# A two-layer encoder trunk in split float32: column strips, float32 attention, a second DMA queue, more raw weight buffers, other groups

## The chip, the cores and the metric

One core of a Trainium2 chip runs the whole program. The metric is the device time of one execution in microseconds (us), lower is better. Engines: PE (TensorE), DVE (VectorE), ACT (ScalarE), POOL (GpSimd) and SP (SyncE, which here only issues DMAs). They run side by side and meet at semaphores.

## What is computed

Two layers of a hybrid encoder on one sequence of 1024 positions with 1024 channels, all float32, then a final RMSNorm. Cut to what matters:

```python
for layer in range(2):
    hn = rmsnorm(h, norm1_g[layer])
    u, q, k, v, gate_a, gate_b = split(hn @ w_in[layer])      # 512, 512, 128, 128, 1024, 1024 columns
    y_a = s5_branch(u, ...)        # bidirectional diagonal state space, 32 groups of 16 channels, then GLU
    y_b = windowed_gqa(q, k, v, sink, bias, mask)   # 8 heads of 64, 2 kv heads, window +-128, blocks of 128
    merged = sigmoid(gate_a) * (y_a @ w_branch_a) + sigmoid(gate_b) * (y_b @ w_branch_b)
    h = h + merged @ w_out[layer]
    hn2 = rmsnorm(h, norm2_g[layer])
    h = h + (silu(hn2 @ w_gate) * (hn2 @ w_up)) @ w_down      # 2816 hidden columns
return rmsnorm(h, final_g)
```

## The kernel before

**Tiling.** Activations lie with channels on the 128 partitions and the sequence in two halves of 512 columns (`HC`). A matrix product is a chain (`chain`, lines 167 to 176): for each 128x128 piece of the weights three matmuls of 512 columns, high weight by high activation (line 174), high by low (175), low by high (176). High and low are the float32r halves of a float32 number; ACT makes the high one by a copy, DVE the low one by a subtraction (`split`, lines 111 and 112; for weights `parts`, lines 162 and 163). A product of two plain float32 tiles is one instruction in the code and two records in the trace.

**Weights.** A granule is one weight tile of up to 128x1024. `fetch` (lines 120, 123) loads it into one of two `raw` buffers, `parts` or `quad_part` (lines 137 to 151) splits it into `whi` and `wlo`. `emit` walks the list of work items in the order of the code and brings the granules ahead of the items that use them; `ahead` fetches up to one granule beyond the one being split. A raw buffer is free again when DVE has made the low half.

**Stages of a layer.** Projections (`pj`), with the S5 tables prepared between them; attention in 16 units (kv head, block of 128 queries): scores (`s`, line 790), a fused add-and-maximum on DVE (793), exponentials on ACT (797), a scaling on DVE, transposes on PE (`pt`, 818), values (`pv`, 830); the S5 recurrence over 16 pairs of groups (`s5x`, 939, and `s5y`, 981 to 984); the GLU (`glu`), the branch products (`br`), `wo`, and the feed-forward part. This last runs in groups of hidden tiles (`GROUPS`): all gate and up products of a group, then 16 down chains (`dn`), which add to `h`. `h` lies in DRAM as `hs` between groups: each down chain loads its piece (line 1205), DVE adds (1210), and the sum is stored again (1212) except in the last group of the last layer, where the squares for the last norm are summed instead. From hidden tile 10 of the first layer and 2 of the second on, gate and up are multiplied as one 2x2 block product with seven instead of eight parts (`quad_items`: `qx`, `qy`, `qv`, `qw`).

**S5 tables.** For each of 2 x 16 pairs `s5_prep_pair` makes the matrices `WB` and `CA` on DVE and, on PE, four transposes (`pswb`, line 628) and 8 float32 matmuls into a 32-partition strip of one PSUM tile (`psE`, lines 642 and 644: four of 112 columns, four of 16). Tables, `u`, gates (`th`), and the S5 output (`s5g`, four DMAs for each pair of pairs, line 1009) go to DRAM and come back later.

**Order.** Every DMA is on SP's queue, loads and stores together, in one order; an issue that waits holds back those behind it. All other tiles are in one pool of 90 slots of 2 KB per partition (`N_SLOTS`), PSUM in 8 tiles of 512 columns. The first items of layer 0 keep the order of the code on PE, DVE and ACT; behind them a scheduler may move instructions within an engine, and it also chooses the slots.

In attention before, queries are held as two tiles for each pair of heads, `qe` and `qo`, with high and low halves of one head on the two halves of the partitions, and keys as `kh` and `kl`, each doubled over both halves, so that a head's scores are two float32r matmuls over 128 rows. The values tile has high and low columns next to each other (`vt`), so that two matmuls for each key block, with the high and low probabilities, give 128 output partitions whose halves ACT and DVE add (lines 832 and 842).

Of the kernel before, what the change touches and what calls it, by code (L numbers as in the profile page):

```python
# [8 lines left out]
F32 = mybir.dt.float32  # L9
# [17 lines left out]
          ((0, 2), (2, 3), (5, 3), (8, 3), (11, 3), (14, 3), (17, 3), (20, 2)))  # L27
# [14 lines left out]
N_SLOTS = 90  # L42
# [4 lines left out]
W_BUFS = 3  # L47
TB_EARLY = 4
# [46 lines left out]
class Trunk:  # L95
# [19 lines left out]
    def fetch(self, g):  # L115
        if isinstance(g, QuadPart):
            if g.kind in "ab":
                i = "ab".index(g.kind)
                r = g.quad.raw[i] = self.pw.tile([P, DM], F32, tag="raw", name="raw", bufs=2)
# [452 lines left out]
    def s5_table_early(self, l, q):  # L572
        self.nc.sync.dma_start(self.sp[l][q][2], self.s5_table(l, q))

    def s5_prep_pair(self, l, q):
# [43 lines left out]
        for g in range(2):  # L619
            dst = bass.AP(tensor=sp[1].tensor, offset=sp[1].offset + g * 256, ap=[[HC, 64], [64 * HC, 2], [1, 256]])  # L620
            nc.sync.dma_start(dst, CA[64 * g:64 * g + 64].rearrange("p (r c) -> p r c", r=2))
# [9 lines left out]
        nc.sync.dma_start(sp[0], WBT)  # L631

        i = q % 4
        if i == 0:
            self.psE = self.PS("psE")
        BD = BD.rearrange("p (q d r m) -> p q d r m", q=4, d=2, r=2)[:, i]
        ca = CA.rearrange("p (r d c) -> p d r c", d=2, r=2)
        E = self.psE[32 * i:32 * i + 32]
        cc = [t.rearrange("p (d q h) -> p d q h", d=2, q=NPAIR)[:, :, q] for t in (p["Cr"], p["Ci"])]
# [3 lines left out]
        for k, (d, r) in enumerate(((0, 0), (0, 1), (1, 0), (1, 1))):  # L643
            nc.tensor.matmul(E[:, 112:128], lhsT=BD[:, d, r], rhs=cc[r][:, d], start=k == 0, stop=k == 3)
        if i == 3:
# [4 lines left out]
            nc.sync.dma_start(self.ed[l][q // 4], es[:, 0:240])  # L650
# [51 lines left out]
    def key_tiles(self, kn, kv, T):  # L702

        nc = self.nc
        s = slice(64 * kv, 64 * kv + 64)
        hh, ll = self.A(f"kh{kv}{T}", F32R), self.A(f"kl{kv}{T}", F32R)
        for o in (slice(0, 64), slice(64, 128)):
            nc.scalar.copy(hh[o], kn[T][s])
        for o in (slice(0, 64), slice(64, 128)):
            nc.vector.tensor_tensor(ll[o], kn[T][s], hh[s].bitcast(F32), SUB)  # L710
        self.kt[kv, T] = (hh, ll)

    def value_tiles(self, vn):
        nc = self.nc
        for T in range(2):
# [3 lines left out]
            for b in range(2):  # L719
                vt = self.A("vt", F32R)  # L720
                o = vt.rearrange("p (k s d) -> p k s d", s=2, d=64)
                src = pt[:, b * 256:(b + 1) * 256].rearrange("p (k d) -> p k d", d=64)
                nc.scalar.copy(o[:, :, 0], src)
                nc.vector.tensor_tensor(o[:, :, 1], src, o[:, :, 0].bitcast(F32), SUB)
                self.vt.append(vt)

    def tile_q(self, l, i, xs=None):
        nc = self.nc
        st = {}

        def done(h, ps):
# [6 lines left out]
            lo, up = slice(0, 64), slice(64, 128)  # L738
            for T in range(2):
                e, o = self.A(f"qe{i}{T}", F32R), self.A(f"qo{i}{T}", F32R)  # L740
                nc.scalar.copy(e[lo], qn[T][lo])
                nc.vector.tensor_tensor(e[up], qn[T][lo], e[lo].bitcast(F32), SUB)
                nc.scalar.copy(o[up], qn[T][up])
                nc.vector.tensor_tensor(o[lo], qn[T][up], o[up].bitcast(F32), SUB)
# [879 lines left out]
```

## Time and profile before

| | us |
|---|---|
| median of 3 runs (2749.10 to 2753.00) | 2750.16 |
| the profiled execution, own time | 2751.03 |
| its span, first to last instruction | 2749.2 |
| PE busy / DVE busy / ACT busy / POOL busy | 2651.0 / 1880.3 / 972.1 / 0.2 |
| mean granted TensorE clock, as a share of 2.4 GHz | 0.983 |
| DMA: bytes moved, mean rate | 365 MB by SP's queue, 134 GB/s |

A PE record's duration is longer than its turn, because matmuls overlap in the array; what counts is the distance from one start to the next. A row's "<-" names what ended the idle time before it.

### The profile page before, as it was taken

Reading aid. Unit: us, or ns where it says so; the run is one execution under the profiler, and the core shown is the slowest. Engines: PE = TensorE matmul, PEld = TensorE weight load, DVE = VectorE, ACT = ScalarE, POOL = GpSimd, SP = SyncE. Lnnn points to the kernel's source line nnn. Section 1 sums busy time; section 2 is a strip of 40 time slices with the busy share of each in tenths; the row PEclk is TensorE's granted clock in tenths of the full one; section 3 lists DMA queues with packets and bytes.
Section 4 is the critical chain, followed back from the end, with each engine's and each line's share of the span. In section 5 each row is a group of like instructions: output and inputs, shape, how many; then the busy total and the mean of one; then the engine's idle time right before and its main releaser. Section 6 shows DMA issues by size and latency. Waiting matters only on the chain.

```text
span 2749.2 us, 35031 instructions
## 1 busy us (share of the span) xinstructions
PE 2651.0 (96%) x12738; PEld 2182.3 (79%) x12738; DVE 1880.3 (68%) x3881; ACT 972.1 (35%) x1829; POOL 0.2 (0%) x4
## 2 busy tenths in 40 slices
PE   8999997899999999999999999999999999999996
PEld 6788876688788888888878888888877888878775
DVE  8977988674965666656675877756377566656656
ACT  5325754432322222222345653343233223212222
POOL 0000000000000000000000000000000000000000
PEclk9999998999999999999999999999999999999998
DMA  3453235354245342553342135534415433543453
GB/s 118 133 164 112 95 113 172 120 202 139 84 125 187 105 147 73 176 169 106 123 167 75 56 108 177 177 122 154 134 65 176 162 103 131 180 161 94 138 173 132
DMA packets 205053, 367.47 MB, mean 134 GB/s; under 512 B 22304, under 2 KB 70688, under 8 KB 204880
## 3 DMA queue, kind: packets, MB, share of 16 engines
q1 hardware_dynamic: 204880, 365.23, 40.4%
q8 instruction: 100, 1.64, 0.2%
q14 instruction: 73, 0.60, 0.1%
HBM read 246.70 MB, written 118.44 MB: 133 GB/s over the span
## 4 chain that ended last, share of the span: by engine, by line
PE 80%; DVE 11%; DMA 5%; ACT 2%; issue 2%; SPq 1%; DVEq 0%; ACTq 0%
PE pj L174 6%; PE pj L175 6%; PE pj L176 6%; PE dn L174 4%; PE dn L175 4%; PE dn L176 4%; DMA raw<-in_w_up 2%; PE qy L187 2%; PE qy L185 2%; PE wo L175 2%; PE wo L174 2%; PE wo L176 2%; PE qy L186 2%; PE qv L187 2%; PE qv L186 2%; PE qv L185 2%
## 5 line engine op out<-in xcount | busy, mean ns | idle before, releaser
L162 ACT CAST whi<-raw 128x1024 fp32r<-128x1024 f32 (+3 forms) x208 | 169.5, 815 | 540.4 <-DMA raw<-in_w_down 130.8
L163 DVE TENSOR_TENSOR wlo<-raw,whi 128x1024 fp32r<-128x1024 f32 (+3 forms) x208 | 193.3, 930 | 196.7 <-ACT whi L162 188.2
L174 PE MATMUL pj<-rah,whi 128*128 128x512 f32 x768 | 308.6, 403 | 7.9 <-DVE sm L793 6.8
L175 PE MATMUL pj<-ral,whi 128*128 128x512 f32 x768 | 303.0, 395 | 3.5 <-DVE ral L112 3.5
L176 PE MATMUL pj<-rah,wlo 128*128 128x512 f32 x768 | 302.0, 394 | 0.0
L1210 DVE TENSOR_TENSOR h<-h,dn 128x512 f32<-128x512 f32 x224 | 151.0, 684 | 139.5 <-PE dn L176 98.3
L174 PEld LDWEIGHTS pj<-rah,whi 128*128 128x128 f32 x768 | 146.1, 190 | 43.3 <-DVE sm L793 8.3
L175 PEld LDWEIGHTS pj<-ral,whi 128*128 128x128 f32 x768 | 146.2, 190 | 35.0 <-DVE ral L112 6.7
L176 PEld LDWEIGHTS pj<-rah,wlo 128*128 128x128 f32 x768 | 145.8, 190 | 31.1
L185 PE MATMUL qx<-rfh,whi 128*128 128x512 f32 x256 | 100.2, 391 | 2.3 <-ACT whi L150 2.3
L187 PE MATMUL qx<-rfh,wlo 128*128 128x512 f32 x256 | 100.3, 392 | 1.0 <-DVE wlo L151 1.0
L186 PE MATMUL qx<-rfl,whi 128*128 128x512 f32 x256 | 100.1, 391 | 0.0
L174 PE MATMUL wo<-mgh,whi 128*128 128x512 f32 x256 | 100.0, 391 | 0.0
L175 PE MATMUL wo<-mgl,whi 128*128 128x512 f32 x256 | 99.7, 390 | 0.1
L176 PE MATMUL wo<-mgh,wlo 128*128 128x512 f32 x256 | 99.7, 389 | 0.0
L967 ACT COPY s5sg<-s5s 64x256 f32<-64x256 f32 x128 | 51.7, 404 | 135.1 <-DVE s5s L962 120.8
L174 PE MATMUL dn<-ffbh,whi 128*128 128x512 f32 x216 | 85.1, 394 | 0.0
L175 PE MATMUL dn<-ffbl,whi 128*128 128x512 f32 x216 | 84.2, 390 | 0.0
L175 PE MATMUL dn<-ffal,whi 128*128 128x512 f32 x216 | 84.2, 390 | 0.0
L797 ACT ACTIVATE x<-x,sm 128x384 f32<-128x384 f32 (+1 forms) x128 | 73.8, 578 | 29.3 <-DVE sm L793 29.3
L176 PE MATMUL dn<-ffah,wlo 128*128 128x512 f32 x216 | 84.1, 389 | 0.0
L174 PE MATMUL dn<-ffah,whi 128*128 128x512 f32 x216 | 84.1, 389 | 0.0
(440 smaller groups left out, 6726.3 us busy)
## 6 DMA issues: line engine op xcount, KB each, us to landing
hs<-h SPq DMA_DIRECT2D x240, 256.0 KB
h<-hs SPq DMA_DIRECT2D x240, 256.0 KB
raw<-in_w_in SPq DMA_DIRECT2D x52, 512.0 KB
raw<-in_w_gate SPq DMA_DIRECT2D x44, 512.0 KB
raw<-in_w_up SPq DMA_DIRECT2D x44, 512.0 KB
g<-th SPq DMA_DIRECT2D x64, 256.0 KB
thr<-g SPq DMA_DIRECT2D x64, 256.0 KB
raw<-in_w_down SPq DMA_DIRECT2D x80, 192.0 KB
```

The source lines that it names most:

```text
L162: nc.scalar.copy(g.hi[:, :n], g.raw[:, :n])
L163: nc.vector.tensor_tensor(g.lo[:, :n], g.raw[:, :n], g.hi[:, :n].bitcast(F32), SUB)
L174: mm(ps, lhsT=wh, rhs=xh, start=k == 0, stop=False)
L175: mm(ps, lhsT=wh, rhs=xl, start=False, stop=False)
L176: mm(ps, lhsT=wl, rhs=xh, start=False, stop=k == n - 1)
L185: mm(ps, lhsT=wh, rhs=xh, start=start and k == 0, stop=False)
L186: mm(ps, lhsT=wh, rhs=xl, start=False, stop=False)
L187: mm(ps, lhsT=wl, rhs=xh, start=False, stop=k == len(xs) - 1)
L797: nc.scalar.activation(ex[h][:, :n], ex[h][:, :n], AF.Exp, scale=-1.0, bias=nm[:, h:h + 1], accum_out=su[:, h:h + 1])
L967: nc.scalar.copy(SG[64 * r:64 * r + 64, g * 256:(g + 1) * 256].rearrange("p (d n) -> p d n", d=2), Sv[64 * g:64 * g + 64, :, r])
L1210: V.tensor_tensor(x, x, ps, ADD)
```

## The change

It has five parts.

- **psE over column strips.** The psE matmuls of a pair are kept back until four pairs are ready; then they are issued together, so that matmuls that follow each other write four different strips of 32 output partitions.
- **Float32 attention.** Queries, keys, values and probabilities stay plain float32, without high and low. Scores of two heads are issued in turn, one on partitions 0 to 63, one on 64 to 127, into two PSUM tiles; values of two heads in turn into output partitions 0 to 63 and 64 to 127. `att_values` ends in two copies of 128x128.
- **Stores through GpSimd.** All stores to DRAM but the bias row and the output go by `nc.gpsimd.dma_start`; loads stay with SP.
- **Four raw buffers.** `raw` has four buffers in place of two, and `ahead` fetches up to three granules beyond the one being split. They take 8 KB more per partition; `N_SLOTS` goes from 90 to 86, which is 8 KB.
- **Other groups in the second layer.** (2, 3, 3, 3, 3, 3, 3, 2) hidden tiles become (2, 2, 3, 3, 3, 3, 3, 3).

```diff
-          ((0, 2), (2, 3), (5, 3), (8, 3), (11, 3), (14, 3), (17, 3), (20, 2)))
+          ((0, 2), (2, 2), (4, 3), (7, 3), (10, 3), (13, 3), (16, 3), (19, 3)))
...
-N_SLOTS = 90
+N_SLOTS = 86
+R_BUFS = 4
...
-        g.raw = self.pw.tile([P, DM], F32, tag="raw", name="raw", bufs=2)
+        g.raw = self.pw.tile([P, DM], F32, tag="raw", name="raw", bufs=R_BUFS)
...
-            self.fetch_to(min(self.split_ + 2, len(self.order)))
+            self.fetch_to(min(self.split_ + R_BUFS, len(self.order)))
...
-        for d, dst, win in ((1, slice(0, 112), slice(16, 128)), (0, slice(128, 240), slice(0, 112))):
-            for r in range(2):
-                nc.tensor.matmul(E[:, dst], lhsT=BD[:, d, r], rhs=ca[:, d, r, win], start=r == 0, stop=r == 1)
+            for d, dst, win in ((1, slice(0, 112), slice(16, 128)), (0, slice(128, 240), slice(0, 112))):
+                for r in range(2):
+                    for k, (bd, ca, _) in enumerate(self.taps):
+                        nc.tensor.matmul(self.psE[32 * k:32 * k + 32, dst], lhsT=bd[:, d, r], rhs=ca[:, d, r, win],
+                                         start=r == 0, stop=r == 1)
...
-            for w in range(2):
-                for a, e in spans:
-                    kk = self.kt[kv, a // 4][w]
-                    nc.tensor.matmul(ps[:, (a - k0) * P:(e - k0) * P], lhsT=q, rhs=kk[:, (a % 4) * P:(a % 4 + e - a) * P],
-                                     start=w == 0 and a == k0, stop=w == 1 and e == k1)
+            for a, e in spans:
+                for j, ps in enumerate(pss):
+                    r = slice(64 * j, 64 * j + 64)
+                    nc.tensor.matmul(ps[:, (a - k0) * P:(e - k0) * P], lhsT=q[r, (3 - oq) * P:(4 - oq) * P],
+                                     rhs=self.kt[kv, a // 4][r, (a % 4) * P:(a % 4 + e - a) * P], start=a == k0, stop=e == k1)
...
-            out.append(self.split(ps, "p"))
+            out.append(self.A("p"))
+            nc.scalar.copy(out[k], ps)
...
-            for w in range(2):
-                nc.tensor.matmul(ps, lhsT=v, rhs=pt[k][w], start=k == 0 and w == 0, stop=k == n - 1 and w == 1)
-        t = self.A("pvl")
-        nc.scalar.copy(t[0:64], ps[64:128])
+            for j in range(2):
+
+                nc.tensor.matmul(ps[64 * j:64 * j + 64, 0:256].rearrange("p (i q) -> p i q", i=2), lhsT=v, rhs=p[:, j],
+                                 start=k == 0, stop=k == n - 1)
...
-            nc.vector.tensor_tensor(y[hp, w], ps[0:64, c], t[0:64, c], ADD)
+            nc.vector.tensor_copy(self.yb[2 * kv + i, T][:, (3 - o) * P:(4 - o) * P], ps[:, i * P:(i + 1) * P])
...
-                nc.sync.dma_start(dst, t[:, g * 256 + k * P:g * 256 + (k + 1) * P])
+                nc.gpsimd.dma_start(dst, t[:, g * 256 + k * P:g * 256 + (k + 1) * P])
...
-                nc.sync.dma_start(self.hs[m, h], x)
+                nc.gpsimd.dma_start(self.hs[m, h], x)
```

On PE, in the projections of layer 0, where the first S5 tables are made. Before, one pair's matmuls stand behind its transposes:

```order
L176 MATMUL pj_1424<-rah,wlo 128x512
L628 MATMUL pswb<-cst,WB 128x128 x4
L642 MATMUL psE<-CA,BD 32x112 x4
L644 MATMUL psE<-Cr,BD 32x16
L644 MATMUL psE<-Ci,BD 32x16
L644 MATMUL psE<-Cr,BD 32x16
L644 MATMUL psE<-Ci,BD 32x16
L174 MATMUL pj_1501<-rah,whi 128x512
```

Now, behind the transposes of the fourth pair:

```order
L177 MATMUL pj_1578<-rah,wlo 128x512
L629 MATMUL pswb<-cst,WB 128x128 x4
L645 MATMUL psE<-CA,BD 32x112 x16
L649 MATMUL psE<-Cr,BD 32x16 x4
L649 MATMUL psE<-Ci,BD 32x16 x4
L649 MATMUL psE<-Cr,BD 32x16 x4
L649 MATMUL psE<-Ci,BD 32x16 x4
L175 MATMUL pj_1669<-rah,whi 128x512
```

The 32 matmuls of four pairs stand in one row, 16 of 112 columns and 16 of 16, and neighbours write different strips.

On PE, in attention of layer 0, one unit's scores. Before (`kh`, `kl` keys, `qe`, `qo` queries of an even and an odd head):

```order
L790 MATMUL s<-kh_2202,qe_714 128x384
L790 MATMUL s<-kl_2203,qe_714 128x384
L790 MATMUL s<-kh_2202,qo_715 128x384
L790 MATMUL s<-kl_2203,qo_715 128x384
L790 MATMUL s<-kh_2202,qe_832 128x384
L790 MATMUL s<-kl_2203,qe_832 128x384
L790 MATMUL s<-kh_2202,qo_833 128x384
L790 MATMUL s<-kl_2203,qo_833 128x384
L818 MATMUL pt<-cst,x 128x128 x8
```

Now (`kk` keys, `qn` queries):

```order
L177 MATMUL pj_2536<-rah,wlo 128x512
L774 MATMUL s<-kk_2157,qn_651 128x384 x2
L774 MATMUL s<-kk_2157,qn_743 128x384 x2
L820 MATMUL pv<-p,vt 64x256 x4
L805 MATMUL pt<-cst,x 128x128 x12
```

Eight float32r matmuls became four float32 ones, in pairs over two halves of the rows.

On SP, in the S5 part of layer 0 (`zd` the stored S5 output, `s5wbt`, `s5ca`, `s5tb`, `s5uk` the loads for one pair). Before:

```order
L919 DMA s5uk<-ud_321 128x2x128
L924 DMA s5uk<-ed_1_183 128x1x128 x2
L1009 DMA zd_324<-s5g 8x16x128 x4
L123 DMA raw<-in_w_glu 128x1024
L914 DMA s5wbt<-sp_8_0_110 128x512
L914 DMA s5ca<-sp_8_1_111 128x512
L914 DMA s5tb<-sp_8_2_112 128x512
L919 DMA s5uk<-ud_322 128x2x128
```

Now:

```order
L904 DMA s5uk<-ud_325 128x2x128
L909 DMA s5uk<-ed_1_183 128x1x128 x2
L124 DMA raw<-in_w_br_a 128x1024
L899 DMA s5wbt<-sp_8_0_110 128x512
L899 DMA s5ca<-sp_8_1_111 128x512
L899 DMA s5tb<-sp_8_2_112 128x512
```

The four stores of `s5g` have left the row; they stand on POOL, where before there was no DMA.

## Rows read from the trace of the kernel before

**Rows 1.** The page, part 1: busy us, share of the span, instructions.
```profile
PE 2651.0 (96%) x12738; PEld 2182.3 (79%) x12738; DVE 1880.3 (68%) x3881; ACT 972.1 (35%) x1829; POOL 0.2 (0%) x4
```
**Rows 2.** Waits of PE, whole span: us in total, times, longest.
```profile
PE s5x L939 <- DMA s5uk<-ud: 15.4, 3, 6.4
PE psn L301 <- DVE sqc L292: 10.5, 3, 6.1
PE qy L185 <- ACT whi L150: 9.3, 9, 2.5
...
PE pj L174 <- DVE sm L793: 6.8, 5, 1.9
...
PE glu L174 <- ACT zp0h L111: 4.1, 1, 4.1
...
PE dn L174 <- ACT whi L162: 3.2, 1, 3.2
```
**Rows 3.** Timeline of PE, psE in layer 0: start, us, records.
```profile
128.34 0.95 PE L642 MATMUL psE<-CA,BD 128*32 128x112 f32 x8
129.13 0.21 PE L644 MATMUL psE<-Cr,BD 128*32 128x16 f32 x2
...
129.46 0.50 PE L174 MATMUL pj<-rah,whi 128*128 128x512 f32 x1
```
**Rows 4.** Timeline, S5 of layer 0: two strips in turn, then full width.
```profile
442.12 1.10 PE L939 MATMUL s5x<-s5uk,s5wbt 128*64 128x128 f32 x16
...
446.24 0.39 PE L983 MATMUL s5y<-s5sg,s5ca 128*128 128x127 f32 x2
...
446.46 0.39 PE L984 MATMUL s5y<-s5sg,s5ca 128*128 128x127 f32 x2
```
**Rows 5.** Timeline of PE, one attention unit of layer 0.
```profile
247.73 0.33 PE L790 MATMUL s<-kh,qe 128*128 128x384 f32 x1
...
249.14 0.39 PE L830 MATMUL pv<-ph,vt 128*128 128x512 f32 x1
...
250.08 1.47 PE L818 MATMUL pt<-cst,x 128*128 128x128 f32 x12
```
**Rows 6.** Timeline, S5 of layer 0: SP's queue and PE.
```profile
445.44 2.54 SPq L1009 DMA_DIRECT2D zd<-s5g  x4
...
450.00 0.38 SPq L919 DMA_DIRECT2D s5uk<-ud  x1
...
455.29 1.98 PE L939 MATMUL s5x<-s5uk,s5wbt 128*64 128x128 f32 x16 [6.43 <-DMA s5uk<-ud]
```
**Rows 7.** Stretches: us, busy PE, PEld, DVE, ACT, POOL, PEclk, DMA share, GB/s.
```profile
450.00:470.00 20.00, 11.13 (x85) 9.27 (x85) 18.19 (x41) 7.62 (x17) 0.00 (x0) 0.79 0.69 223
...
2080.00:2110.00 30.00, 23.41 (x86) 17.51 (x85) 22.75 (x36) 10.26 (x19) 0.00 (x0) 0.89 0.81 271
```
**Rows 8.** Timeline, end of a down stage of layer 1: SP, DVE, PE.
```profile
2649.45 0.46 SPq L120 DMA_DIRECT2D raw<-in_w_up  x1
...
2651.49 6.90 SPq L1212 DMA_DIRECT2D hs<-h  x3
...
2656.03 0.69 DVE L137 TENSOR_TENSOR sm<-raw 128x512 f32<-128x512 f32 x1 [2.83 <-DMA raw<-in_w_up]
...
2658.66 0.50 PE L185 MATMUL qy<-tt1h,whi 128*128 128x512 f32 x1 [2.51 <-ACT whi L150]
```
**Rows 9.** Timeline, the last down group and the last norm.
```profile
2712.74 1.05 PE L301 MATMUL psn<-ones,sqc 128*128 128x1 f32 x8 [2.84 <-DVE sqc L292]
...
2718.34 2.07 PE L324 MATMUL psn<-cst,rs 128*128 128x128 f32 x8 [2.51 <-DVE rs L87]
...
2733.78 1.84 PE L301 MATMUL psn<-ones,sqc 128*128 128x1 f32 x8 [6.06 <-DVE sqc L292]
```
**Rows 10.** Groups of DVE: line, shapes, count, busy us, mean ns, idle before.
```profile
L112 DVE TENSOR_TENSOR pl<-pt,ph 128x512 fp32r<-128x512 f32 x88 | 55.5, 683 | 1.1 <-ACT ph L111 0.4
L842 DVE TENSOR_TENSOR yb<-pv,pvl 64x128 f32<-64x128 f32 x128 | 36.0, 282 | 3.8 <-ACT pvl L832 1.7
```

More of the change, by code (lines that the diff above doesn't have):

```diff
@@ L118, in fetch @@
                 i = "ab".index(g.kind)
-                r = g.quad.raw[i] = self.pw.tile([P, DM], F32, tag="raw", name="raw", bufs=2)
+                r = g.quad.raw[i] = self.pw.tile([P, DM], F32, tag="raw", name="raw", bufs=R_BUFS)
                 self.nc.sync.dma_start(r, g.quad.src[i])
             return
-        g.raw = self.pw.tile([P, DM], F32, tag="raw", name="raw", bufs=2)
+        g.raw = self.pw.tile([P, DM], F32, tag="raw", name="raw", bufs=R_BUFS)
         self.nc.sync.dma_start(g.raw[:, :g.n], g.src)
@@ L630, in s5_prep_pair @@
         nc.scalar.copy(WBT, ps)
-        nc.sync.dma_start(sp[0], WBT)
+        nc.gpsimd.dma_start(sp[0], WBT)
         i = q % 4
         if i == 0:
-            self.psE = self.PS("psE")
[L636 to L639, printed above, removed]
-        for d, dst, win in ((1, slice(0, 112), slice(16, 128)), (0, slice(128, 240), slice(0, 112))):
-            for r in range(2):
-                nc.tensor.matmul(E[:, dst], lhsT=BD[:, d, r], rhs=ca[:, d, r, win], start=r == 0, stop=r == 1)
-        for k, (d, r) in enumerate(((0, 0), (0, 1), (1, 0), (1, 1))):
-            nc.tensor.matmul(E[:, 112:128], lhsT=BD[:, d, r], rhs=cc[r][:, d], start=k == 0, stop=k == 3)
+            self.taps = []
+        cc = [t.rearrange("p (d q h) -> p d q h", d=2, q=NPAIR)[:, :, q] for t in (p["Cr"], p["Ci"])]
+        self.taps.append((BD.rearrange("p (q d r m) -> p q d r m", q=4, d=2, r=2)[:, i],
+                          CA.rearrange("p (r d c) -> p d r c", d=2, r=2), cc))
+        if i == 3:
+            self.psE = self.PS("psE")
+            for d, dst, win in ((1, slice(0, 112), slice(16, 128)), (0, slice(128, 240), slice(0, 112))):
[3 more added lines that the diff above has]
+                                         start=r == 0, stop=r == 1)
+            for n, (d, r) in enumerate(((0, 0), (0, 1), (1, 0), (1, 1))):
+                for k, (bd, _, cc) in enumerate(self.taps):
+                    nc.tensor.matmul(self.psE[32 * k:32 * k + 32, 112:128], lhsT=bd[:, d, r], rhs=cc[r][:, d],
+                                     start=n == 0, stop=n == 3)
         if i == 3:
@@ L702, in key_tiles @@
     def key_tiles(self, kn, kv, T):
-        nc = self.nc
-        s = slice(64 * kv, 64 * kv + 64)
-        hh, ll = self.A(f"kh{kv}{T}", F32R), self.A(f"kl{kv}{T}", F32R)
+        kk = self.kt[kv, T] = self.A(f"kk{kv}{T}")
         for o in (slice(0, 64), slice(64, 128)):
[L708 to L711, printed above, removed]
+            self.nc.scalar.copy(kk[o], kn[T][64 * kv:64 * kv + 64])
     def value_tiles(self, vn):
@@ L718, in value_tiles @@
                 nc.tensor.transpose(pt[:, b * P:(b + 1) * P], vn[T][:, b * P:(b + 1) * P], self.ident)
[L719 to L725, printed above, removed]
+            self.vt.append(self.A("vt"))
+            nc.scalar.copy(self.vt[T], pt)
     def tile_q(self, l, i, xs=None):
-        nc = self.nc
         st = {}
@@ L763, in done @@
             store[i, h] = self.pd.tile([P, HC], F32, name=f"g{l}_{m0}_{i}_{h}")
-            nc.sync.dma_start(store[i, h], th)
+            nc.gpsimd.dma_start(store[i, h], th)
         return self.proj(l, m0 + i, done)
@@ L836, in att_values @@
                 self.yb[2 * kv + i, T] = self.A(f"yb{kv}{i}")
-        w = slice((3 - o) * P, (4 - o) * P)
-        for h in range(4):
-            y = self.yb[2 * kv + h // 2, T]
-            hp = slice(64 * (h % 2), 64 * (h % 2) + 64)
-            c = slice(h * P, (h + 1) * P)
-            nc.vector.tensor_tensor(y[hp, w], ps[0:64, c], t[0:64, c], ADD)
+        for i in range(2):
+            nc.vector.tensor_copy(self.yb[2 * kv + i, T][:, (3 - o) * P:(4 - o) * P], ps[:, i * P:(i + 1) * P])
     def att_pairs(self, kv):
```

48 lines of the change are left out of this document (20 added, 28 removed).

## The prediction

> **What bounds the kernel now.** I read the page first: PE is busy for 2651.0 us of a span of 2749.2, DVE for 1880.3, ACT for 972.1, POOL for nothing [rows 1]. So an edit pays where it shortens PE's own work or takes away one of the few waits of PE; work taken from DVE or ACT pays only where PE waits for it. The waits of PE come next [rows 2]. The reader is to see that they are short and scattered: 15.4 us for loads of the S5 part, 10.5 for the sums of squares in the norms, 9.3 and 3.2 for weights of the feed-forward part, 6.8 for DVE in attention, 4.1 for the first GLU product. Then I read the timeline at each place that the diff touches, to see what one instruction costs and which queue or engine stands behind each wait.
>
> **The change part by part.** *psE.* One pair takes from 128.34 to 129.46, 1.12 us: 0.79 for four float32 matmuls of 112 columns, 0.33 for four of 16 [rows 3]. The 32 pairs take 36 us, nearly all on PE's path. What strips give can be read from the S5 part [rows 4]. The full-width float32 matmuls start 0.22 us apart for 127 columns. The eight of s5x, with 128 columns in two strips of 64 by turns, are over in 1.10 us including the drain of the last record (about 0.28), so they start some 0.11 apart: two strips in turn halve the price. Each matmul is two records that go to the same strip one behind the other, so if records start in the order in which they are written, only neighbours overlap, and four strips give no more than a halving. I take half of the 112-column part, 32 x 0.39 = 12.6 us, and a quarter of the small ones, 2.6 us, since these may be held by a cost per instruction. That is -15. The bounds are 0 and, with four strips at once, three quarters of 36, -27.
>
> The Trainium skill ("TensorE: Matmul & The Clock Gate", Part 3) says that tiles of the array work at the same time, and gives 2.38 times for three column strips. By that the saving would be about -21, an estimate; [rows 4] show two strips only and can't decide between this and a halving.
>
> *Scores.* Eight float32r matmuls of 384 columns take from 247.73 to 249.14, 1.41 us [rows 5]. Now there are four float32 matmuls. By [rows 4] a float32 matmul costs 0.22 us for 127 columns, so 0.66 for 384; four one after the other take 2.66, and 1.33 if the two halves of the rows work at the same time. There are 32 units with 88 key blocks, 29 full units in all: +36 us at one end, -2.5 at the other. No row of this trace shows two row halves in turn. The nearest is two column strips with the same kind of matmul in the same alternation [rows 4], so I take the overlap, -3 with the units that were split over two key tiles, and keep +36 as a rival.
>
> *Values.* Four matmuls of 512 columns take from 249.14 to 250.08, 0.235 each, two for each key block: 0.47 [rows 5]. Two float32 ones of 256 columns are 0.44 each, in turn on two column strips of 64 as in [rows 4]: 0.44 for both. That is 88 x 0.03, -2.5 us; without overlap it would be +36, which rows 4 speak against.
>
> *DVE and ACT in attention.* DVE loses the low halves of the probabilities, 55.5 us, and the 128 additions, 36.0 us, for 64 copies of about 0.28 [rows 10], and some splits of queries and keys. This is hidden behind PE except where projections wait for the maximum, 6.8 us over both layers [rows 2]. I take -4 (0 to -8): the last unit, with little beside it, keeps its chain.
>
> *Stores out of SP's queue.* In the S5 part of layer 0 the four zd stores sit in front of the next loads; their issue alone takes 2.54 us, the u load goes out at 450.00, and PE stands still for 6.43 us until 455.29 [rows 6]. Three such waits make 15.4 us [rows 2], and after them PE runs at half clock for a while (PEclk 0.79 in this stretch [rows 7]). With the stores on POOL the loads are not held. But DVE is busy for 18.19 of 20 us there while PE does 11.13 [rows 7]: DVE is next late, and most of the wait can become a wait for it. I take -10 (0 to -25).
>
> *Four raw buffers.* At the end of a down stage the load of an up tile goes out at 2649.45 and SP is then held for 6.90 us by three hs stores; DVE waits for the tile until 2656.03 and PE for its high half until 2658.66 [rows 8]. With fetches two granules earlier and no stores before them, the 9.3 and 3.2 us [rows 2] should go, and a few us at half clock behind them. I take -15 (-6 to -20).
>
> *Groups.* In the last group two tiles make a chain of six matmuls, 1.4 us by [rows 5], while DVE has an addition and a sum of 0.69 each [rows 8] and a split of weights for it. So DVE falls behind, and PE waits 2.84, 2.51 and 6.06 us [rows 9]. With three tiles a chain is 2.1 us. The first wait goes; the second is the short chain of the norm and stays; the third shrinks by the five chains behind it, 5 x 0.7. That is -6 (0 to -9). The price is a second group of two tiles early in the layer. The first such group has PE busy for 23.41 of 30 us at a DMA share of 0.81 [rows 7], because 16 pieces of h are loaded and stored in little time. A second one may lose as much: I take +4 (0 to +10).
>
> *POOL as a queue.* POOL does nothing now [rows 1], so no row prices a store there. SP needs 2.54 us for four [rows 6]. Where a store is soon read back, as S5 output before the GLU (4.1 us [rows 2], in each layer its own hand-over), a later landing is paid in full. I take +3 (-2 to +8). The 4 slots fewer I cost at nothing: attention gives up more tiles than that; where slots are short elsewhere, that belongs to the third rival.
>
> The sum is -15 -3 -2.5 -4 -10 -15 -6 +4 +3 = -48.5 us. It is made against the profiled execution's 2751.0, which stands 0.9 above the median of the runs: 2702 us.
>
> **The rivals.** *Row halves don't overlap.* Scores cost +36 instead of -3: 2702 + 39 = 2741. For it: no row shows them. Against it: the strips of rows 4.
>
> *GpSimd's queue is the bound.* This one ends slower. In a down stage with three tiles PE gives a sum every 2.1 us, with two tiles every 1.4. Nine groups of three and two of two store 16 pieces each. If a store holds POOL for c us, the queue falls behind by 144 x (c - 2.1) + 32 x (c - 1.4); the pieces hold their slots, and the chains behind wait. It eats the 48.5 us at c = 2.25; at 2.5 it costs 93 and gives 2795. Against it: SP issues such stores in well under 1 us (a quarter of 2.54 [rows 6]); POOL would have to be four times as slow. The rule of the Trainium skill that speaks for it is in "SBUF — State Buffer" (SBUF: two separate sides): DMAs from GpSimd have their descriptors written by software, which is locked out while DVE runs a mode that uses two ports. No row here shows it.
>
> *The waits stay.* DVE takes the place of the loads in S5, the DMA rate that of the queue in the down stages (share 0.81 [rows 7]), and fewer slots give something back. Then there remain -15 -3 -2.5 -2 of PE's work and attention, and -1.5 of the groups: -24, 2727.
>
> *More strips, no DVE bound.* Four strips overlap (12 more) and the S5 waits go whole (8 more): 2682.
>
> **How the numbers follow.** The forecast has 50 of 100 (its own range 2685 to 2722), the waits that stay 20, the row halves 12, the better case 9, GpSimd's queue 9. The range from 2676 to 2744 takes in all but the last and the edges of two others. About 0.2%, 5.5 us, is what a measurement of this kernel can tell from no change. Of the row halves' case a third lies within or above that. So faster 0.86, same 0.04, slower 0.10.
>
> **What would show it.** psE: the 32 matmuls of four pairs in about 2.6 us instead of 4.5. Scores: four matmuls in 1.3 us, not 2.7; values 0.44 for a key block. S5: no wait of s5x for s5uk, in its place waits of s5y for DVE's states. Feed-forward: no qy or dn wait for whi. The end: a third psn wait near 2.5 us. POOL: a distance between hs stores set by DVE, not by POOL itself. The prediction is wrong if PE's records in scores start 0.32 us apart without pairs, if POOL's issues run back to back through the down stages, or if the S5 part of layer 0 is as long as before.

## Result and profile after

| | before | after |
|---|---|---|
| median, us | 2750.8 (4 runs, 2749.1 to 2753.0) | 2681.3 (4 runs, 2678.4 to 2683.7) |
| ratio, 95% interval | | 0.9746 [0.9729, 0.9763] |
| span of the profiled execution | 2749.2 | 2680.9 |

The change saves 69.5 us where 48.5 were forecast; the time lies inside the range (2676 to 2744) and near its lower end. The page of after, parts 1 and 5; [rows 1] has the first line of before:

```profile
PE 2607.8 (97%) x12914; PEld 2119.6 (79%) x12914; DVE 1765.1 (66%) x3673; ACT 929.9 (35%) x1761; POOL 295.0 (11%) x524
...
L1197 POOL DMA_DIRECT2D hs<-h x192 | 104.5, 544 | 875.8 <-DVE h L1195 849.2
```

PE lost 43 us of busy time and DVE 115. POOL holds 192 stores of `h` for 0.54 us each, and nearly all its idle time in front of them ends with DVE's addition: DVE sets their distance, not POOL. That rules out the rival of GpSimd's queue, which needed 2.25 us for a store.

Some of PE's longest waits in after (us in total, times, longest), to be held against [rows 2]:

```profile
PE s5x L924 <- DVE s5a L934: 10.6, 1, 10.6
...
PE s5x L924 <- DVE s5a L935: 5.5, 1, 5.5
PE psn L302 <- DVE sqc L293: 5.4, 2, 3.0
PE glu L175 <- ACT zp3h L112: 4.0, 1, 4.0
PE qy L186 <- ACT whi L151: 3.5, 1, 3.5
```

The waits of s5x have another name and the same size, 16.1 against 15.4 us. The waits for split weights (12.5 us) shrank to one of 3.5, and the squares wait twice instead of three times.

Where the time went, by stage. Every border is the first or last start of a tile's matmuls in PE's timeline (first and last score, first GLU product, last `wo`, last down product):

| stage, us | before | after | difference |
|---|---|---|---|
| start to first score, layer 0 (half of the S5 tables) | 233.6 | 216.8 | -16.8 |
| attention, layer 0 | 144.2 | 142.1 | -2.1 |
| S5, layer 0: last score to first GLU product | 150.1 | 141.2 | -8.9 |
| GLU, branches, `wo`, layer 0 | 157.9 | 161.6 | +3.7 |
| feed-forward, layer 0 (other half of the tables) | 728.4 | 714.3 | -14.1 |
| layer 1 up to its last `wo` | 606.6 | 597.0 | -9.6 |
| feed-forward, layer 1 | 706.6 | 688.9 | -17.7 |
| last down product to the end | 21.8 | 19.0 | -2.8 |

psE in after, PE's timeline (start, us, records), where [rows 3] had one pair at a time:

```profile
144.00 0.97 PE L645 MATMUL psE<-CA,BD 128*32 128x112 f32 x32
...
144.98 0.28 PE L649 MATMUL psE<-Ci,BD 128*32 128x16 f32 x8
145.19 0.50 PE L175 MATMUL pj<-rah,whi 128*128 128x512 f32 x1
```

Four pairs are over in 1.19 us, where one alone took 1.12. Over the 32 pairs, from start to start, psE fell from 36.0 to 9.9 us: the bound that the prediction gave as -27, not the halving that it took.

One attention unit in after, beside [rows 5]:

```profile
260.78 1.56 PE L774 MATMUL s<-kk,qn 64*128 64x384 f32 x8
262.27 1.52 PE L820 MATMUL pv<-p,vt 128*64 128x256 f32 x12
263.72 1.53 PE L805 MATMUL pt<-cst,x 128*128 128x128 f32 x12
```

The four scores take 1.49 us from their start to the next tile's (1.41 before), the values of three key blocks 1.45, 0.48 a block (0.47 before). So both kinds of halves do overlap; without that the scores alone would take 2.66, an estimate from the 0.66 us of one [rows 4]. But PE wins nothing by them.

The end, PE's timeline, beside [rows 9]:

```profile
2643.65 0.95 PE L302 MATMUL psn<-ones,sqc 128*128 128x1 f32 x8
2649.32 1.16 PE L325 MATMUL psn<-cst,rs 128*128 128x128 f32 x8 [2.51 <-DVE rs L88]
...
2665.33 1.02 PE L302 MATMUL psn<-ones,sqc 128*128 128x1 f32 x8 [3.02 <-DVE sqc L293]
2668.78 2.08 PE L325 MATMUL psn<-cst,rs 128*128 128x128 f32 x8 [2.43 <-DVE rs L88]
```

The first wait (2.84) is gone, the second stays at 2.51, the third fell from 6.06 to 3.02.

### The profile page after: what moved, and what is told of

Same layout as the page of the kernel before. It is cut to its first block, busy times and chain, and to the rows that moved or that the text cites. A ratio compares the mean times of both kernels' runs of the same rounds, so it can differ in the third digit from the quotient of the medians.

```text
span 2680.9 us, 35600 instructions
## 1 busy us (share of the span) xinstructions
PE 2607.8 (97%) x12914; PEld 2119.6 (79%) x12914; DVE 1765.1 (66%) x3673; ACT 929.9 (35%) x1761; POOL 295.0 (11%) x524
## 4 chain that ended last, share of the span: by engine, by line
PE 87%; DVE 7%; DMA 3%; ACT 1%; issue 1%; SPq 0%; POOL 0%; DVEq 0%; ACTq 0%
PE pj L175 6%; PE pj L176 6%; PE pj L177 6%; PE dn L175 6%; PE dn L176 5%; PE dn L177 5%; PE wo L175 2%; PE qy L186 2%; PE qy L188 2%; PE wo L176 2%; PE wo L177 2%; PE qy L187 2%; PE qv L186 2%; PE qv L187 2%; PE qv L188 2%; PE qx L187 2%
## 5 line engine op out<-in xcount | busy, mean ns | idle before, releaser
L1197 POOL DMA_DIRECT2D hs<-h x192 | 104.5, 544 | 875.8 <-DVE h L1195 849.2
L780 DVE CUSTOM_DVE_ANT_0 x<-s,bias,nsink 128x384 f32<-128x384 f32 (+1 forms) x128 | 67.7, 581 | 89.2 <-PE s L774 89.2
```

The costliest lines, as they stand in the source:

```text
L780: V.tensor_tensor_reduce(out=x[:, :n], in0=ps[:, :n], in1=self.bias[hd][:, bo:bo + n], op0=ADD, op1=ALU.min, scale=-1.0, scalar=self.nsink ...
L1197: nc.gpsimd.dma_start(self.hs[m, h], x)
```

## Experiments

Stages of the runs, us, from the profiled executions, borders as above (e1 varies its order from place to place, so its stages aren't listed):

| | before | after | e2 | e3 | e4 | e5 | e6 | e7 | e8 | e9 | e10 | e11 | e12 |
|---|---|---|---|---|---|---|---|---|---|---|---|---|---|
| to first score | 233.6 | 216.8 | 230.8 | 216.1 | 216.3 | 216.5 | 216.1 | 230.7 | 217.0 | 216.7 | 216.4 | 216.1 | 216.6 |
| attention 0 | 144.2 | 142.1 | 142.1 | 142.1 | 142.0 | 142.0 | 142.1 | 142.1 | 142.0 | 125.9 | 125.9 | 125.8 | 125.9 |
| S5 0 | 150.1 | 141.2 | 141.7 | 141.2 | 142.9 | 144.0 | 141.6 | 143.7 | 136.7 | 151.1 | 144.3 | 142.7 | 147.3 |
| GLU to `wo` 0 | 157.9 | 161.6 | 161.7 | 161.5 | 159.0 | 159.6 | 162.3 | 157.6 | 156.4 | 157.5 | 156.3 | 157.4 | 157.5 |
| feed-forward 0 | 728.4 | 714.3 | 727.9 | 717.7 | 712.6 | 717.9 | 714.5 | 734.7 | 712.7 | 712.7 | 712.4 | 713.8 | 711.7 |
| layer 1 to `wo` | 606.6 | 597.0 | 593.8 | 593.8 | 596.0 | 600.7 | 597.0 | 600.6 | 593.8 | 593.8 | 593.8 | 593.4 | 597.6 |
| feed-forward 1 | 706.6 | 688.9 | 689.1 | 696.3 | 689.7 | 707.5 | 685.8 | 707.3 | 690.8 | 692.1 | 688.0 | 682.4 | 683.0 |
| end | 21.8 | 19.0 | 19.8 | 19.0 | 18.0 | 18.1 | 22.4 | 21.2 | 19.0 | 19.7 | 19.2 | 18.7 | 18.1 |

Two rows show how far a stage moves with no edit in it. Layer 1 up to its `wo` takes 597.0 us in after and 593.8 in e2 and e9. The difference lies in its first projections, before the first score: 68.6 us at a mean granted clock of 0.95 in after, 65.4 at 1.00 in the two others. And the feed-forward part of layer 1, with the same code in after, e2, e8 and e9, takes 688.9 to 692.1. So 3 us in one stage of one pair of runs show nothing by themselves.

### e1: the order of the strips

In the scores `j` is the half of the rows, in the values the half of the output; `kv` is the kv head, `ks` the strips that are issued in turn.

```diff
+            sets = {1: ((0, 1), (2, 3)), 2: ((0,), (1,), (2,), (3,))}.get(q // 4, ((0, 1, 2, 3),))
+            for ks in sets:
...
-                    for k, (bd, ca, _) in enumerate(self.taps):
+                        for k in ks:
+                            bd, ca, _ = self.taps[k]
...
+        ops = [(i, a, e, j) for i in range(2) for a, e in spans for j in range(2)]
+        if kv:
+            ops.sort(key=lambda o: o[3])
...
+        ops = [(k, j) for k in range(n) for j in range(2)]
+        if kv:
+            ops.sort(key=lambda o: o[1])
```

> The changed kernel, with the issue order of the strips varied from place to place inside one program, so that one trace prices them. psE of layer 0 (four batches of four pairs, 32 matmuls each): batch 1 four strips in turn as in the changed kernel, batch 2 two strips in turn and then the other two, batch 3 strip by strip, batch 4 as batch 1. Scores and values of the first kv head in turn as in the changed kernel; of the second, the two heads on one half of the rows come first, then the two on the other half, and the values of one output half come for all key blocks before the other half. Theory, turns: neighbours in the queue that use different strips overlap, and a float32 matmul's two records do not stand in the way. Then batches 1 and 4 take 1.2 us, batch 2 about 2.3, batch 3 about 4.5 (4 x 1.12, as four pairs before); scores of a full unit 1.3 us for the first kv head and 2.0 for the second (three turns of 0.66 in place of two), values of three key blocks 1.3 and 2.2 (five turns of 0.44 in place of three). Rival, free overlap: the array takes whatever strip is free from further back, and batching alone is enough; then batches 2 and 3 take 1.2 to 1.5 too, and both kv heads cost the same. Second rival, the forecast's: only neighbouring records overlap; then four strips can't take less than 2.2, and batches 1 and 2 cost the same.

2695.9 us, a single run; what counts here is one trace's prices. PE's timeline of e1: the first psE row of batch 2 and the product that follows the batch, the same of batch 3, then one unit of the first and one of the second kv head:

```profile
174.34 0.96 PE L648 MATMUL psE<-CA,BD 128*32 128x112 f32 x16
...
176.40 0.50 PE L175 MATMUL pj<-rah,whi 128*128 128x512 f32 x1
...
200.31 0.95 PE L648 MATMUL psE<-CA,BD 128*32 128x112 f32 x8
...
204.19 0.50 PE L175 MATMUL pj<-rah,whi 128*128 128x512 f32 x1
...
273.95 1.56 PE L778 MATMUL s<-kk,qn 64*128 64x384 f32 x8
275.44 1.52 PE L826 MATMUL pv<-p,vt 128*64 128x256 f32 x12
...
342.99 1.57 PE L778 MATMUL s<-kk,qn 64*128 64x384 f32 x8
344.48 2.00 PE L826 MATMUL pv<-p,vt 128*64 128x256 f32 x12
```

The scores of a unit whose keys lie in two tiles, of the first kv head and of the second:

```profile
244.29 1.58 PE L778 MATMUL s<-kk,qn 64*128 64x256 f32 x16
...
331.87 2.34 PE L778 MATMUL s<-kk,qn 64*128 64x128 f32 x16
```

Four strips in turn take 1.19 us, two 2.06, strip by strip 3.88, each from the first start of the batch to the start of the next product. The price goes with the number of strips in turn, and the batching by itself brings little (4 x 1.12 = 4.48 against 3.88). That is the theory of turns, and the halving is out. But turns alone are not all: scores in the order half A, A, B, B cost the same as A, B, A, B (1.57 and 1.56 us), where three turns would have made 2.0, and the values by halves cost 2.00, less than the expected 2.2. A scheduler may move instructions here, but in the program of e1 PE's order in these units is that of the code. So a matmul on a free half of the array also starts ahead of one that waits in front of it, as far as one matmul back at least. It doesn't reach four back, since four on A and then four on B cost 2.34 us where in turn they cost 1.58, nor eight, or batch 3 would cost 1.2.

### e2: psE pair by pair

```diff
-                    for k, (bd, ca, _) in enumerate(self.taps):
-                        nc.tensor.matmul(self.psE[32 * k:32 * k + 32, dst], lhsT=bd[:, d, r], rhs=ca[:, d, r, win],
-                                         start=r == 0, stop=r == 1)
...
+        E = self.psE[32 * i:32 * i + 32]
...
+                nc.tensor.matmul(E[:, dst], lhsT=BD[:, d, r], rhs=ca[:, d, r, win], start=r == 0, stop=r == 1)
```

> The changed kernel with the psE matmuls issued pair by pair again, each pair in its own strip, as in the kernel before; all else as changed. Theory: the strips take psE from 36.0 to 9.9 us on PE and all of it lies on the path, so undoing it costs 26 us: 2681 + 26 = 2707, ratio to the kernel before 0.984. The forecast's step gave 15 (to 2696); and if PE would wait for something else in that time (tables that DVE is late with, or loads) less than 10 would come back, 2690.

2710.3 us, ratio to before 0.9848 [0.9828, 0.9867]. That is 28 us above after by the ratios, 26 by the spans. The stages show it where the tables are made, +14.0 up to the first score and +13.6 in layer 0's feed-forward part. All 26 us of psE lay on the path.

### e3, e4, e5: raw buffers and the stores' queue

e3 has the first of these edits, e4 the second (at every store), e5 both.

```diff
-R_BUFS = 4
+R_BUFS = 2
...
-                nc.gpsimd.dma_start(self.hs[m, h], x)
+                nc.sync.dma_start(self.hs[m, h], x)
```

> The changed kernel with two raw buffers in place of four and fetches one granule ahead; 86 slots as changed. Theory of the forecast: early fetches take away PE's waits for split weights in the feed-forward part (qy and dn for whi, 12.5 us in the kernel before) and some half clock behind them; undoing costs 15 us (6 to 20), 2681 + 15 = 2696, and qy and dn waits for whi come back. Rival: what held the loads was the stores in SP's queue ahead of them; with these on GpSimd two buffers are enough, and undoing costs 0 to 4 us, 2681 to 2685.

> The changed kernel with every store back in SP's queue; four raw buffers as changed. Theory of the forecast: the waits of s5x for loads in the S5 part of layer 0 come back (15 us in the kernel before) in place of its waits for DVE (16 us in the changed kernel), so the part gets only a little longer, and GpSimd's own price goes: net +7 us, 2688. Rival one: stores in SP's queue also hold the raw loads at the ends of the down stages, and four buffers don't cover it: +20, 2701, with qy or dn waits for whi. Rival two: stores on GpSimd bring nothing but a later hand-over of the S5 output to the GLU (waits for zp0h and zp3h, 5.9 us in the changed kernel): -5, 2676.

> The changed kernel with both queue parts undone: two raw buffers and every store in SP's queue; psE, attention, groups and 86 slots as changed. The S5 part of layer 0 (end of the last score to the first GLU product) took 150 us before, 141 in the changed kernel, 141 with two buffers alone undone and 143 with the stores alone undone. Theory, either is enough: the two parts cover for each other, so with both undone the part goes back to 150 us, s5x waits longer for its loads, and the total is 8 (raw buffers in the feed-forward part) + 9 above the changed kernel, 2698 to 2700. Rival: the 9 us come from the attention part (DVE and ACT with less behind them, more free slots) or from DVE being the bound in every case; then the part stays at 141 to 143 and the total is 2688 to 2691.

| | two raw buffers | four |
|---|---|---|
| stores on SP | e5: 2706.7, 0.9837 [0.9822, 0.9851] | e4: 2679.4, 0.9737 [0.9723, 0.9752] |
| stores on GpSimd | e3: 2689.8, 0.9774 [0.9759, 0.9789] | after: 2681.3, 0.9746 [0.9729, 0.9763] |

e3 lies between its theory (2696) and its rival (2681 to 2685), e4 between its theory (2688) and its second rival (2676). Both parts together are worth 25 us (0.0091 of 2751). Four buffers alone bring all of it (27); the stores alone bring 17; beside four buffers the stores bring nothing that these runs show. So they cover for each other, as e5's theory had it, but not in the S5 part, which it named: there the four kernels take 141.2 to 144.0 us, all below 150. Most of it, 18.6 us, lies in the feed-forward part of layer 1: 707.5 us with both undone, 696.3 and 689.7 with one, 688.9 with none. PE's waits of e5, then of e3:

```profile
PE s5x L924 <- DMA s5uk<-ud: 16.0, 4, 6.1
PE qx L186 <- ACT whi L151: 8.7, 2, 4.8
PE qy L186 <- ACT whi L151: 8.0, 8, 1.4
...
PE dn L175 <- ACT whi L163: 4.2, 3, 2.3
```

```profile
PE s5x L924 <- DMA s5uk<-ud: 16.8, 2, 10.6
...
PE qy L186 <- ACT whi L151: 5.6, 1, 5.6
```

The waits of qx, qy and dn for split weights are 20.9 us in e5. And s5x waits 16 to 17 us in all of them (in e4 13.0, and 4.4 for `zd`), under whatever name.

### e6: the old groups

```diff
-          ((0, 2), (2, 2), (4, 3), (7, 3), (10, 3), (13, 3), (16, 3), (19, 3)))
+          ((0, 2), (2, 3), (5, 3), (8, 3), (11, 3), (14, 3), (17, 3), (20, 2)))
```

> The changed kernel with the groups of the second layer as before, (2, 3, 3, 3, 3, 3, 3, 2). Forecast: the last group of three tiles saves 6 us at the end, the second group of two costs 4 early; undoing costs 2 us, 2683, with psn waits for the squares 3 and 6 us long again at the end. Rival: the second small group costs nothing, since with four raw buffers its loads are early; then undoing costs 6 to 9, 2687 to 2690. Other rival: the small group costs more than the end gives, and undoing is a gain, 2676 to 2680.

2681.4 us, ratio 0.9747 [0.9732, 0.9762]: no difference. Behind the last down product the old groups are 3.4 us slower (22.4 against 19.0), where PE waits longer for the squares again (5.4 us in after). Up to there they are 3.1 faster (685.8 against 688.9), which agrees with the forecast's early price but is no more than this part's spread:

```profile
PE psn L302 <- DVE sqc L293: 10.2, 3, 5.7
```

### e7: float32 attention alone

The kernel before with `key_tiles`, `value_tiles`, `tile_q`, `att_scores`, `att_transpose` and `att_values` of the changed kernel, and nothing else of it.

> The kernel before with the float32 attention alone (keys, values, queries, scores, probabilities, values; 90 slots, two raw buffers, stores in SP's queue, psE by pair, old groups). Forecast's steps: scores -3, values -2.5, less waiting for DVE -4, together -9.5: 2750 - 9.5 = 2741, and the S5 part of layer 0 as long as before (150 us from the last score to the first GLU product). Rival: the lighter attention also leaves DVE and ACT less behind when the S5 part begins, and the S5 part's 9 us come from here: 2732, S5 part 141 us. Rival, PE's work alone: only the matmuls get shorter, the waits stay: -5, 2745.

2738.7 us, ratio 0.9955 [0.9940, 0.9970], -12.4. In layer 0 attention itself gets 2.1 us shorter; 2.9 come before it, and 6.4 behind it, in the S5 part; layer 1 up to its `wo` gets 6.0 shorter. Two windows of 20 us around the last unit, before and e7 (length; busy PE, PEld, DVE, ACT, POOL; PEclk, DMA share, GB/s):

```profile
380.00:400.00 20.00, 17.10 (x77) 13.66 (x76) 13.29 (x37) 9.75 (x25) 0.00 (x0) 0.83 0.47 159
```

```profile
375.00:395.00 20.00, 19.49 (x123) 15.37 (x121) 14.25 (x39) 8.89 (x22) 0.00 (x0) 1.00 0.43 145
```

Before, PE stood for 2.9 us at the last unit's chain and then ran part of this stretch at the lower of its two clock levels, 1.2 GHz (mean 0.83); in e7 0.5 us of that wait is left and the clock stays at 1.00. Not explained: e7 gives 6 us back in layer 0's feed-forward part (734.7 against 728.4); PE's waits account for 3.0 of them.

### e8: the S5 part, and a releaser that misleads

In after the profile names DVE as what s5x waits for. SP's queue says otherwise. Timeline of after, SP and PE:

```profile
404.26 1.17 SPq L909 DMA_DIRECT2D s5uk<-ed  x2
421.55 0.34 SPq L124 DMA_DIRECT2D raw<-in_w_br_a  x1
...
423.41 0.38 SPq L904 DMA_DIRECT2D s5uk<-ud  x1
...
428.94 1.97 PE L924 MATMUL s5x<-s5uk,s5wbt 128*64 128x128 f32 x16 [5.51 <-DVE s5a L935]
```

From 405.4 to 421.55 SP issued nothing: a weight load stood at its head and waited for a raw buffer, and the loads of the next pair stood behind it. The u load went out at 423.41 and s5x started 5.5 us later; in before that took 5.3 [rows 6]. That DVE ends at that moment looks like a coincidence: in e3, where the S5 part takes the same time, the waits of s5x carry the load's name. SP's waits in this part, first of before (418 to 500 us), then of after (395 to 475 us):

```profile
SPq L1009 <- DVE s5g L1004: 25.1, 4, 15.2
SPq L123 <- DVE wlo L163: 4.0, 1, 4.0
```

```profile
SPq L124 <- DVE wlo L164: 34.7, 2, 18.6
```

Before, SP stood 25.1 us because the zd stores waited for DVE's result, not for the 2.54 us that their issue takes. In after a weight load that waits for DVE's split has taken their place. Both hang on DVE, which has a stall of its own. DVE's timeline of after:

```profile
432.23 0.68 DVE L981 SCALAR_TENSOR_TENSOR s5w<-s5g,s5y 128x512 f32<-128x512 f32 x1
434.39 0.69 DVE L989 SCALAR_TENSOR_TENSOR s5g<-s5g,s5y 128x512 f32<-128x512 f32 x1 [1.47 <-ACT s5g L982]
434.99 0.68 DVE L932 TENSOR_TENSOR s5a<-s5x,s5tb 128x512 f32<-128x512 f32 x1
```

DVE makes ACT's input and at once waits for ACT's tanh, with the next pair's states behind it. e8 puts them in between:

```diff
-            if end:
-                self.item(lambda i=i - 2: self.s5_store(i, st))
             if out:
                 self.item(lambda i=i - 1: self.s5_output(l, i, st))
             if on:
                 self.item(lambda q=2 * j: self.s5_states(l, q, st[q]))
+            if end:
+                self.item(lambda i=i - 2: self.s5_store(i, st))
...
+        if l == 0:
+            self.dve_order = range(first, len(self.seq))
```

In that range of items, layer 0's S5 part, DVE keeps the order of the code. The moved store and the kept order were not run apart.

> The changed kernel with another order on DVE in the S5 part of layer 0: the last multiplication of the S5 output (line 989) stands behind the states of the next pair and no longer directly behind the product that ACT's tanh waits for (line 981), and DVE keeps the order of the code there. In the changed kernel DVE stands still for 1.47 us between the two, eight times, in a part in which it is busy 18 of 20 us. Theory, DVE is the bound of this part: it gets shorter by up to 8 x 1.47 = 12 us, the waits of s5x for DVE (16 us) shrink to 4 to 6, total 2669 to 2673. Rival, the loads are as late as DVE: the waits get the name of s5uk or s5tb and the total stays within 3 us of 2681. Rival, the S5 output's later store delays the GLU: waits for zp0h and zp3h grow by what is won.

2674.1 us, ratio 0.9721 [0.9705, 0.9737], 7 below after. By the profiled execution, the fastest of its four, the S5 part is 4.5 us shorter and the part behind it 5.2 (the wait for zp3h is gone), not the 12 of DVE's eight stalls. The waits of s5x now carry the loads' name, and SP is held as before; PE's and SP's waits of e8:

```profile
PE s5x L925 <- DMA s5uk<-ud: 13.3, 2, 7.0
```

```profile
SPq L124 <- DVE wlo L164: 29.5, 2, 16.9
```

So theory and first rival are both half right: DVE's stalls cost something, and the loads behind the held weight load are as late. To issue the weight load behind the S5 loads, or from another queue, was not tried.

### e9 to e12: work for PE in the S5 part, and a faster version

e9 has the first two edits. e10 has these, e8's, and the groups (0, 2), (2, 3), (5, 3), (8, 3), (11, 2), (13, 3), (16, 3), (19, 3). e11 and e12 have all three edits shown, the seven groups among them, and e8's; e12 has its stores on SP.

```diff
-                left = self.attention_items(l, keys, q23, ga, 1, tail_items)
+                left = self.attention_items(l, keys, q23, ga, 0.75, tail_items)
...
-                left = self.s5_items(l, left + bb, 1.6)
+                left = self.s5_items(l, left + bb, 2)
...
-          ((0, 2), (2, 2), (4, 3), (7, 3), (10, 3), (13, 3), (16, 3), (19, 3)))
+          ((0, 2), (2, 4), (6, 4), (10, 3), (13, 3), (16, 3), (19, 3)))
```

> The changed kernel with four of the 16 projections that fill layer 0's attention left for its S5 part (0.75 instead of 1 for each unit, and 2 instead of 1.6 items for each step of S5). Theory: in the S5 part DVE is the bound (busy 18 of 20 us in places) and PE stands for about 20 us, while attention, now lighter on DVE (93 us busy of 137), is bound by PE. Four projections are 4 x 24 matmuls x 0.227 = 22 us: attention gets shorter by these, the S5 part stays nearly as long, since they fall into PE's waits (16 us for DVE and what runs at half clock behind them): 2681 - 15 = 2666 (2662 to 2670), and the waits of s5x for DVE or for loads fall under 5 us. Rival, DVE isn't the only bound and S5's loads or the tail of the part are late whatever PE does: the S5 part grows by the whole 22 us and the total stays at 2679 to 2683. Second rival, attention needs its filling: units without a projection wait for the exponentials, waits of pt and pv appear, and half of the gain is lost, 2674.

2668.8 us, ratio 0.9693 [0.9666, 0.9721]. Attention gets 16 us shorter, and the S5 part only 10 longer, although four projections are 22 us of work for PE (an estimate, 96 matmuls at 0.227). The total is what the theory said; the waits of s5x are not, with 11.0 us where under 5 were expected.

> The changed kernel with three things: the later S5 store on DVE (2674 alone), four projections moved from attention to S5 in layer 0, and the second small group of the second layer in the middle, (2, 3, 3, 3, 2, 3, 3, 3), since the group of two right behind the first one costs 3.1 us up to the last down chain and the last group of three saves 3.5 behind it. Theory: the S5 part gets shorter in DVE's time and PE has work in it, together 12 + 8 us, and the groups give 3: 2681 - 20 = 2661 (2655 to 2666). Rival, the two S5 edits take away the same waits: one of them alone gives all, 2668 to 2671 with the groups. Rival, a small group costs its 3 us wherever it stands: 3 more.

2659.6 us, ratio 0.9664 [0.9641, 0.9687]: the two S5 edits add up. The feed-forward part takes 688.0 us with the small group in the middle and 688.9 to 692.1 with it second, too little to tell whether its place matters.

> The same, with seven groups in the second layer, (2, 4, 4, 3, 3, 3, 3), in place of eight. There are 16 down chains less, and as many loads, additions and stores of h less; PE's matmuls stay the same. Theory: no second small group and less traffic, 3 us less than eight groups with the small one right behind the first: about as e10 or 1 to 2 below. Rival, four hidden tiles hold 16 slots and more beside the 32 of the sums, 86 slots are too few, and loads of weights or h wait for slots: 5 to 15 us above e10, with waits of qx, qy or dn in the second layer.

2651.7 us, ratio 0.9634 [0.9612, 0.9656], 30 us below after. The feed-forward part takes 682.4, 5.6 less than with the eight groups of e10 and more than the expected 3, and no wait for slots shows. The S5 part of after and of e11 (windows as above):

```profile
420.00:440.00 20.00, 14.48 (x101) 12.26 (x101) 17.96 (x39) 6.67 (x15) 4.72 (x8) 0.83 0.88 279
440.00:460.00 20.00, 14.41 (x108) 11.64 (x104) 18.24 (x40) 8.21 (x17) 2.48 (x5) 0.98 0.19 55
```

```profile
420.00:440.00 20.00, 18.70 (x131) 15.89 (x132) 19.55 (x43) 9.54 (x20) 4.62 (x8) 0.91 0.56 169
440.00:460.00 20.00, 17.98 (x136) 14.64 (x135) 19.66 (x45) 9.60 (x20) 2.52 (x5) 1.00 0.62 200
```

In e11 DVE has no time left there, and PE works for 18 of 20 us instead of 14.

> The version with seven groups, the moved projections and the later S5 store (2651.7, ratio 0.9634), with every store back in SP's queue; four raw buffers. With only this part undone in the changed kernel the time was 2679.4 against 2681.3, no difference. Theory, four raw buffers make the place of the stores indifferent: 2648 to 2655. Rival, with DVE's order mended and PE filled the loads are what is late in the S5 part (waits of s5x for s5uk were 2.4 us in the version with seven groups), and stores of the S5 output in front of them cost again: 2658 to 2665, s5x waits for s5uk or zd over 8 us. Second rival, stores are a little better on SP (the GLU gets its input earlier, no second queue): 2640 to 2647.

2660.4 us, ratio 0.9662 [0.9649, 0.9675], 8 us slower than e11 by the ratios, 9 by the medians. The time is that of the first rival. In the S5 part, 4.6 us longer, PE stands before s5x for 9.3 us instead of 4.9. Another 4.2 lie in layer 1 up to its `wo`, but 2.5 of these in its first projections, where the mean granted clock is 0.97 against 1.00. The wait that the rival named, over 8 us for s5uk or `zd`, is not there under that name: the profile gives 2.6 us of it to the load and 5.0 to nothing that it shows. SP's longest wait from 380 to 480 us, of e12 and of e11:

```profile
SPq L995 <- DVE s5g L990: 25.9, 6, 5.8
```

```profile
SPq L124 <- DVE wlo L164: 50.5, 5, 12.9
```

So with DVE in order and PE filled the stores on GpSimd are worth some 8 us, 2.5 of them where only the clock differs, and nothing in e4. Why is not shown: SP's queue is held in e12 by the `zd` stores, and in e11 even longer by a weight load.

## Why the prediction was right, and where not

| step | forecast | measured | from |
|---|---|---|---|
| psE | -15 | -26 | e2 |
| scores, values on PE | -5.5 | about +1 | PE's distances from start to start, all units |
| DVE and ACT relieved in attention | -4 | -13 | e7, less the line above |
| stores, raw buffers, POOL's price | -10 -15 +3 | -25 | e5 |
| groups, end and early | -6 +4 | -3.4 +3.1 | e6 |

The measured parts make -63. The time fell inside the range partly because errors went both ways: psE and the relief of DVE gave 20 us more than forecast, scores and values 6 less. Some 6 us of the 69.5 have no part; each part is only known to 4 or 5 us, and psE, queues and groups were taken out of the changed kernel, attention put into the old one.

**psE.** The term was mis-sized. Its rows [rows 3, 4] were read rightly; what failed is the argument that two records to one strip leave only neighbours to overlap. The Trainium skill ("TensorE: Matmul & The Clock Gate", Part 3) was nearer with 2.38 times for three strips, against the forecast's two; here four strips gave 36.0 / 9.9 = 3.6 times. The same Part says that matmuls start in the order of the program; e1's scores and values by halves speak against that (1.57 us where starts in order would make 2.0).

**Scores and values.** The overlap was right and the rival of row halves (2741) is out. The small gain was not there: the estimate 4 x 0.66 / 2 left out 0.16 us a unit, which the row shows beyond it, and that of the values 0.13 (1.45 against 3 x 0.44).

**Relief of DVE.** Right in sign, but the forecast had a third of it. The step said that the last unit keeps its chain; it was just there that the two splits and additions fell away, and with them went 2.4 us of a wait and a stretch at the lower clock. The S5 part behind it is 6.4 us shorter in e7, which the prediction had in no term of attention.

**Stores and raw buffers.** Their sum was right (-22 forecast, -25 measured), the split was not; that the sum came out is luck. The prediction took four buffers and a free queue as two gains in two places; they are mostly one gain, in the feed-forward part, and either brings more than half of it. Its sign for the S5 part, that this may not be as long as before, was met for another reason: of the 8.9 us there, attention brings 6.4 (e7) and the queues 2.8 (144.0 in e5, 141.2 in after). In the S5 part it read 2.54 us of issue where SP's waits show 25.1, and it named DVE as next late; the wait came back under DVE's name, at its old size, but through a weight load in the stores' old place. [Rows 6] alone, without SP's own waits, could not tell this.

**Groups.** Right in kind: first wait gone, second kept, third near 2.5 (3.0). The end gave half of the forecast (3.4 of 6). The early group's price, 3.1 of the forecast 4, is no larger than the spread of its stage.

**Rivals.** The case of the better end, 2682, comes nearest to the time, by its first half only: four strips overlap, the S5 waits do not go.

## What to carry over

When small float32 matmuls write different column strips, issue as many strips in turn as there are; one program with a batch of each order gives the price of each. A queue that is freed of one held issue is worth what the next held issue in it leaves, so read the queue's own waits and not only the engine's, and price two edits on one queue together and apart. Where DVE bounds a part, PE's work that is moved into it costs less there than it saves in the part that it leaves (10 against 16 us in e9).

## What the runs showed of the hardware

- 32 float32 matmuls into four strips of 32 output partitions took 1.19 us with four strips in turn, 2.06 with two, 3.88 strip by strip (e1).
- A matmul on a free half of the array starts ahead of an earlier one that waits for the other half, over one matmul but not over four: scores A, A, B, B took 1.57 us, A, B, A, B 1.56; four on A and then four on B took 2.34, in turn 1.58 (e1).
- A store's issue on POOL takes nearly the same time at every place, while DVE is busy for 66% of the span. Tile view of after, duration min/median/max in ns, first and last start:

```profile
L1197 POOL DMA_DIRECT2D hs<-h x192: 539/542/588, 788.7 to 2567.5; - x192
```

and the page's part 6, KB each and us from issue to landing:

```profile
hs<-h POOLq DMA_DIRECT2D x240, 256.0 KB, 5.0
h<-hs SPq DMA_DIRECT2D x240, 256.0 KB, 5.0
```

The starvation that the Trainium skill warns of ("SBUF — State Buffer", SBUF: two separate sides) shows in neither: stores through GpSimd land as fast as loads of the same size through SP. No run shows whether DVE was in a mode that uses two ports beside these stores, so the rule itself is not tested.
